# When four finished rows are normalised during the last matrix product, and which sum each later row's norm follows

## The chip, the cores and the metric

The kernel runs on one core of one Trainium2 chip. TensorE (PE) multiplies matrices into PSUM banks, VectorE (DVE), ScalarE (ACT) and GpSimd (POOL) work on SBUF tiles, SyncE (SP) and ACT issue the stores. Each engine executes its own instruction list in order and waits on semaphores of the others. The metric is device time in microseconds (us) of the whole program.

## The reference

Two blocks over 1024 tokens of width 1024 are computed one after the other; the second ends in a wide feed-forward product and a norm over each row:

```
h = h + jnp.square(jax.nn.relu(m @ w_up[l])) @ w_down[l]
...
h = rms_norm(h, norm_final)

def rms_norm(x, g):
    xf = x.astype(jnp.float32)
    y = xf * lax.rsqrt(jnp.mean(xf * xf, axis=-1, keepdims=True) + EPS)
    return (y * g.astype(jnp.float32)).astype(x.dtype)
```

Only the end matters here: the sums into h for the last quarter of `w_down`, and the final norm.

## The kernel before

The output h lies in SBUF as `X`, eight row tiles (t = 0 to 7, called rows here) of 128 tokens by 1024 columns, each in two column halves (ch = 0 and 1). The product with `w_down` is done in seven sub-products for each of four parts of its inner dimension (loop over `c`); each sub-product goes to four PSUM banks, 128 by 512 each, one for each row of a half of the tokens. A float32 operand is split into a high and a low part: `whi` by ACT (L118, a cast), `wlo` by POOL (L119, a subtraction), and three matmuls (L108, L110, L111) are done for each pair of blocks. In `times` a bank takes 12 matmuls; with `by_t` set, as in the last two sub-products, one bank is finished after the other and the banks of the last sub-product are the same four as those of the one before.

`into(banks, h, ch, done)` adds four banks to `X` (L2034, on DVE). In the last part `done` says that a half row is complete, and `half_done` then squares it and adds up the squares on ACT into `fin` (L1987), and multiplies it in place by the gains `nf` on POOL (L1989). Only half ch = 0 of row 7 is not multiplied there.

`finish(t, n)` takes n rows that are complete: DVE adds the two halves' sums of squares (L1994) and works out the reciprocal root by Newton steps, a chain of small instructions on 128 by n elements that each need the one before: L141 (`hx`), L124 (`r`), then three rounds of `w` and `r`. For n = 4 a round has three instructions (L130, L131, L132), for n = 1 two (L128, L132). ACT then scales each row (L1999) and SP stores it. Row 7 is scaled half by DVE (L2002), half by ACT (L2005), and stored from SP and ACT.

The last part's order is: rows 0 to 3, half 1 (whose half 0 was done earlier); rows 4 to 7, half 1; rows 4 to 7, half 0. The recording layer (`tc`) sets the order of the instructions on each engine; `tc.issue_after(ins)` gives the instructions inside it a place behind `ins`. How the instructions of two steps interleave on DVE and ACT is decided there, and is read from the built instruction lists.

Of the kernel before, what the change touches and what calls it, by code (L numbers as in the profile page):

```python
# [22 lines left out]
NT = T // P  # L23
# [7 lines left out]
def fused_kernel(tc, a, out, stop=None, dbg=None):  # L31
# [85 lines left out]
    def split_evac(hi, lo, src, lo_eng=None):  # L117
        nc.scalar.copy(out=hi, in_=src)  # L118
        return (lo_eng or nc.vector).tensor_tensor(out=lo, in0=src, in1=f(hi), op=ALU.subtract)  # L119
# [18 lines left out]
    def rsqrt(ss, n, rows=P):  # L138

        hx, r, w_ = small3(ss.shape[-1])  # L140
        nc.vector.tensor_scalar(out=hx[:rows], in0=ss[:rows], scalar1=0.5 / n, scalar2=0.5 * EPS, op0=ALU.mult,  # L141
                                op1=ALU.add)
        newton(hx[:rows], r[:rows], w_[:rows])
        return r
# [75 lines left out]
    added, loads, made = [None], [None], [None]  # L220
# [7 lines left out]
    def load_d(dst, w, j, n, c=0, qs=(0, 2)):  # L228

        for i in range(2):  # L230
            q = 4 * c + qs[i]
            loads[:] = [nc.sync.dma_start(out=dst[i], in_=w[:, q:q + 2, j, n * 512:n * 512 + 512])]
        return dst
# [9 lines left out]
    def split_into(t_, parts):  # L243

        for i in range(2):
            made[:] = [split_evac(t_[:, 2 * i:2 * i + 2, :], t_[:, 4 + 2 * i:6 + 2 * i, :], parts[i])]
        return t_
# [15 lines left out]
    def banks4():  # L263
        return [bank() for _ in range(4)]
# [264 lines left out]
    with lay:  # L529
# [267 lines left out]
        for h in range(2):  # L797
# [8 lines left out]
            for i in range(4):  # L806
                t = 4 * h + i
# [35 lines left out]
    with ExitStack() as ph:  # L843
# [191 lines left out]
        def load_x(h, ch):  # L1035
            for t in range(4 * h, 4 * h + 4):
                nc.sync.dma_start(out=X.at(t, ch), in_=d_x1[t][:, ch * 512:ch * 512 + 512])
# [108 lines left out]
        for n, ks in enumerate(((), (), (), (0, 1, 2), (3, 4), (5, 6), (7,), ())):  # L1146
            t = [n % 4]
# [21 lines left out]
        for k in range(KT):  # L1169
            ps = turned(X.x[4:], k)  # L1170
            h, l = x2.at(k, slice(NM + 512, TM))
# [7 lines left out]
        last = scaled  # L1179
# [231 lines left out]
    with ExitStack() as ph:  # L1411
# [65 lines left out]
        class Head:  # L1477
# [145 lines left out]
            def finish(self, hf):  # L1623
                hh, y = self.hh, self.t["y", hf]
                tp = pst.tile([P, 512], F32, name="tp")
                for ch in range(4):
                    nc.tensor.transpose(tp[:, ch * P:(ch + 1) * P], y[:, ch * P:(ch + 1) * P], ident)
                sl = slice(hf * H, hf * H + H)
                oh_ = gp.tile([P, H], F32, name="oh")
                nc.vector.scalar_tensor_tensor(out=oh_, in0=tp, scalar=gn[:, hh:hh + 1], in1=self.t["gs", 0][:, sl],  # L1630
                                               op0=ALU.mult, op1=ALU.mult)
                if hh < 3:
                    nc.sync.dma_start(out=d_hg[hh][:, sl], in_=oh_)
                else:
                    split_evac(*oo.at(7, sl), oh_)
# [53 lines left out]
        last = []  # L1689
        for hh in range(3):  # L1690
# [6 lines left out]
            last = head.ends()  # L1697
# [54 lines left out]
    with ExitStack() as ph:  # L1752
# [106 lines left out]
        for n, ks in enumerate(((), (), (0, 1, 2), (3, 4), (5, 6), (7,), (), ())):  # L1859
            t = [n % 4]  # L1860
# [29 lines left out]
    def load_a(n):  # L1890
        if n < len(seq):
            c, s_ = seq[n]
            nc.sync.dma_start(out=blocks[n % 3], in_=d_u[s_][:, 4 * c:4 * c + 4, :])
# [77 lines left out]
    with ExitStack() as ph:  # L1971
        bb = ph.enter_context(tc.tile_pool(name="bb", bufs=4, reuse_waits="tile"))
        X = ph.enter_context(tc.tile_pool(name="xpool3", bufs=1, reuse_waits="tile")).tile([P, NT, D], F32, name="X3")
        ba = ph.enter_context(tc.tile_pool(name="ba", bufs=1, side="right", reuse_waits="tile"))
        blocks.append(ba.tile([P, 4, 512], F32, name="ub"))
        nf = ba.tile([P, D], F32, name="nf")
        fin = {}

        def half_done(t, ch):

            g = t if t >= 4 else 0
            if g not in fin:
                fin[g] = st.tile([P, 8], F32, name="fin", bufs=5)
            csl = slice(ch * 512, ch * 512 + 512)
            i = 4 * ch + (t if t < 4 else 0)
            junk = st.tile([P, 1024], BF16, name="junk", bufs=1)
            nc.scalar.activation(out=junk[:, csl], in_=X[:, t, csl], func=AF.Square, accum_out=fin[g][:, i:i + 1])  # L1987
            if (t, ch) != (NT - 1, 0):
                nc.gpsimd.tensor_tensor(out=X[:, t, csl], in0=X[:, t, csl], in1=nf[:, csl], op=ALU.mult)  # L1989

        def finish(t, n):

            ss = fin[t]
            nc.vector.tensor_tensor(out=ss[:, :n], in0=ss[:, :n], in1=ss[:, 4:4 + n], op=ALU.add)  # L1994
            r = rsqrt(ss[:, :n], D)
            for i in range(n):
                tsl = slice((t + i) * P, (t + i + 1) * P)
                if t < NT - 1:
                    nc.scalar.activation(out=X[:, t + i, :], in_=X[:, t + i, :], func=AF.Copy, scale=r[:, i:i + 1])  # L1999
                    nc.sync.dma_start(out=out[tsl, :], in_=X[:, t + i, :])  # L2000
                else:
                    nc.vector.scalar_tensor_tensor(out=X[:, t, :512], in0=X[:, t, :512], scalar=r, in1=nf[:, :512],  # L2002
                                                   op0=ALU.mult, op1=ALU.mult)
                    nc.sync.dma_start(out=out[tsl, :512], in_=X[:, t, :512])
                    nc.scalar.activation(out=X[:, t, 512:], in_=X[:, t, 512:], func=AF.Copy, scale=r)  # L2005
                    nc.scalar.dma_start(out=out[tsl, 512:], in_=X[:, t, 512:])

        def load_w21(c):
            return load_d([bb.tile([P, 2, 512], F32, name="wb") for _ in range(2)], wd, 1, 0, c)

        def load_x(h, ch):
            for t in range(4 * h, 4 * h + 4):
                nc.sync.dma_start(out=X[:, t, ch * 512:ch * 512 + 512], in_=d_x[t][:, ch * 512:ch * 512 + 512])

        def split_n(n):
            t_ = split_into(xt.tile([P, KT, 512], F32R, name=("xh0", "xl0", "xl1")[n % 3]),
                            [blocks[n % 3][:, 2 * i:2 * i + 2, :] for i in range(2)])
            load_a(n + 3)
            return t_

        w21 = load_w21(0)
        w12, w22 = load_w2(0)

        store(loads[0].ins)
        load_x(0, 0)
        load_a(2)
        load_x(0, 1)
        load_x(1, 1)
        load_x(1, 0)

        def into(banks, h, ch, done=False):
            for t in range(4):
                dst = X[:, 4 * h + t, ch * 512:ch * 512 + 512]
                added[:] = [nc.vector.tensor_tensor(out=dst, in0=dst, in1=banks[t], op=ALU.add)]  # L2034
                if done:
                    half_done(4 * h + t, ch)
                    if h and not ch:
                        finish(4 * h + t, 1)

        def operands(n, b_):  # L2040
            return split_n(n), split_b(b_)


        ops = operands(0, w11)
        for c in range(NCH):
            n, last = 7 * c, c == NCH - 1
            B, A_ = banks4(), banks4()
            times(B, *ops, True)
            ops = operands(n + 1, w21)
            less(w12, w12, w22)  # L2050
            into(B, 0, 0)
            times(A_, *ops, True)
            less(w11, w11, w12)
            ops = operands(n + 2, w11)
            into(A_, 0, 0, last)
            times(B, *ops, False)
            less(w21, w21, w11)
            less(w11, w22, w11)
            ops = operands(n + 3, w11)
            into(B, 0, 1)  # L2060
            C = banks4()
            times(C, *ops, True)
            ops = operands(n + 4, w22)
            if not last:
                w11 = load_w11(wd, c + 1)
                w21_ = load_w21(c + 1)
            if c == NCH - 2:
                nc.sync.dma_start(out=nf, in_=a["norm_final_2"].partition_broadcast(P))
            into(C, 1, 1)
            times(C, *ops, False)  # L2070
            ops = operands(n + 5, w12)
            if not last:
                w12, w22 = load_w2(c + 1)
            into(C, 0, 1, last)
            times(B, *ops, False, last)
            ops = operands(n + 6, w21)
            into(B, 1, 1, last)
            if last:
                with tc.issue_after(added[0].ins):
                    finish(0, 4)  # L2080
            times(B, *ops, False, last)
            if not last:
                w21 = w21_
                ops = operands(n + 7, w11)
            into(B, 1, 0, last)
# [26 lines left out]
```

## Time and profile before

| what | value |
|---|---|
| median of 3 runs | 2329.97 us (2328.25 to 2332.85) |
| profiled execution, its time | 2328.69 us |
| its span, first to last instruction | 2326.9 us |
| PE busy | 2258.1 us (97%), 11782 matmuls |
| DVE busy | 1520.7 us (65%) |
| ACT busy | 1033.2 us (44%) |
| POOL busy | 735.0 us (32%) |
| mean granted TensorE clock | 0.993 |

The profiled execution is 1.28 us below the median and 1.79 us longer than its span. Busy shares are means over the whole program; the change touches the last 35 us alone, so the timeline of that stretch is what is read below. In a row of the timeline stand the start (us from the span's start), the duration of the group, engine, line, operation, output and inputs, shapes, the number of instructions merged in the row, and in brackets the engine's idle time before it with what ended it.

### The profile page before, as it was taken

What the parts mean: (1) busy time and instruction counts of PE and PEld (TensorE: products, weight loads), DVE (VectorE), ACT (ScalarE), POOL (GpSimd) and SP (SyncE); (2) the same over time, 40 slices, a digit from 0 to 9 for tenths busy, and PEclk for the clock granted to TensorE, in tenths of its full rate; (3) what the DMA queues carried; (4) which work ended last, traced back from release to release, by engine and by line L of the source; (5) the groups of instructions that cost most, each with busy time, mean ns of one, the idle gap of its engine ahead of it and who ended that gap; (6) DMA issues with size and microseconds to landing.
All of it is one profiled execution on the core that took longest, in us unless ns stands there. A gap on an engine that the chain in (4) does not pass through costs nothing.

```text
span 2326.9 us, 32033 instructions
## 1 busy us (share of the span) xinstructions
PE 2258.1 (97%) x11782; PEld 1902.9 (82%) x11782; DVE 1520.7 (65%) x2768; ACT 1033.2 (44%) x1943; POOL 735.0 (32%) x513
## 2 busy tenths in 40 slices
PE   7999999989999999999999999999999999999997
PEld 6888888767787888878988888888878888878886
DVE  5577786798698354553265746759895444787775
ACT  5355552643356354453233232423565555533334
POOL 2112133344501442431312112121024444544455
PEclk9999999999999999999999999999999999999999
DMA  4312113423362311211111111358245444754231
GB/s 144 75 28 55 28 35 108 142 75 123 113 246 101 93 44 50 56 64 42 55 46 55 42 55 51 131 185 300 89 147 194 152 151 159 276 217 163 100 127 73
DMA packets 249581, 255.17 MB, mean 110 GB/s; under 512 B 61193, under 2 KB 183135, under 8 KB 245585
## 3 DMA queue, kind: packets, MB, share of 16 engines
q1 hardware_dynamic: 240608, 235.48, 31.3%
q10 hardware_dynamic: 8224, 16.00, 1.8%
q0 software_dynamic: 592, 1.65, 0.3%
q8 instruction: 93, 1.52, 0.3%
q14 instruction: 64, 0.52, 0.1%
HBM read 181.26 MB, written 69.46 MB: 108 GB/s over the span
## 4 chain that ended last, share of the span: by engine, by line
PE 61%; DVE 10%; issue 3%; DMA 3%; ACT 2%; SPq 0%; POOL 0%; DVEq 0%; ACTq 0%; POOLq 0%
PE mm L110 18%; PE mm L111 18%; PE mm L108 18%; PE A L1564 2%; PE PT L1328 1%; DVE sum L226 1%; DVE xl L119 1%; PE S L1305 1%; PE tp L1584 1%; DVE s L1317 1%; DVE X L2034 0%; DVE r L132 0%; DMA wb<-in_w_down_dram 0%; DVE wlo L119 0%; DVE z L226 0%
## 5 line engine op out<-in xcount | busy, mean ns | idle before, releaser
L108 PE MATMUL mm<-xh,whi 128*128 128x512 f32 (+2 forms) x1616 | 622.6, 386 | 12.1 <-DVE z L226 4.8
L110 PE MATMUL mm<-xl,whi 128*128 128x512 f32 (+2 forms) x1616 | 616.2, 381 | 0.0
L111 PE MATMUL mm<-xh,wlo 128*128 128x512 f32 (+2 forms) x1616 | 613.0, 379 | 0.2 <-POOL wlo L80 0.2
L80 POOL TENSOR_TENSOR wlo<-wraw,whi 128x1024 fp32r<-128x1024 f32 (+1 forms) x99 | 233.7, 2364 | 856.7 <-ACT whi L79 672.7
L108 PEld LDWEIGHTS mm<-xh,whi 128*128 128x128 f32 x1616 | 306.2, 190 | 70.4 <-DVE z L226 5.6
L111 PEld LDWEIGHTS mm<-xh,wlo 128*128 128x128 f32 x1616 | 306.3, 190 | 58.4 <-POOL wlo L80 0.5
L110 PEld LDWEIGHTS mm<-xl,whi 128*128 128x128 f32 x1616 | 306.5, 190 | 50.6
L111 PE MATMUL mm<-whi,xl 128*128 128x512 f32 (+1 forms) x752 | 271.2, 361 | 0.0
L79 ACT CAST whi<-wraw 128x1024 fp32r<-128x1024 f32 (+1 forms) x99 | 101.2, 1023 | 253.3 <-PE mm L110 139.0
L110 PE MATMUL mm<-wlo,xh 128*128 128x512 f32 (+1 forms) x560 | 196.8, 351 | 2.7 <-POOL wlo L80 1.4
L108 PE MATMUL mm<-whi,xh 128*128 128x512 f32 (+1 forms) x560 | 196.5, 352 | 1.8 <-DVE x L527 1.0
L108 PE MATMUL mm<-whi,xl 128*128 128x512 f32 x416 | 162.2, 390 | 1.8 <-DVE X L2034 1.8
L110 PE MATMUL mm<-wlo,xl 128*128 128x512 f32 x416 | 162.1, 390 | 1.2 <-DVE wlo L119 1.2
L111 PEld LDWEIGHTS mm<-whi,xl 128*128 128x128 f32 x752 | 141.7, 188 | 21.6
L276 POOL TENSOR_TENSOR wlo<-raw,whi 128x1024 fp32r<-128x1024 f32 (+1 forms) x59 | 123.0, 2087 | 114.4 <-ACT whi L275 111.7
L110 PEld LDWEIGHTS mm<-wlo,xh 128*128 128x128 f32 x560 | 105.7, 189 | 17.8 <-POOL wlo L80 2.0
L108 PEld LDWEIGHTS mm<-whi,xh 128*128 128x128 f32 x560 | 105.7, 189 | 16.7 <-DVE x L527 1.4
L276 POOL TENSOR_TENSOR wlo<-wraw,whi 128x1024 fp32r<-128x1024 f32 (+1 forms) x28 | 71.9, 2569 | 120.2 <-ACT whi L275 85.9
L2034 DVE TENSOR_TENSOR X<-X,mm 128x512 f32<-128x512 f32 x112 | 73.1, 681 | 37.8 <-PE mm L111 37.8
L1313 DVE CUSTOM_DVE_ANT_0 s<-S,bi 128x400 f32<-128x400 f32 x64 | 34.5, 571 | 95.2 <-PE S L1305 95.2
L108 PEld LDWEIGHTS mm<-whi,xl 128*128 128x128 f32 x416 | 78.1, 188 | 19.2 <-ACT whi L118 1.8
L226 DVE TENSOR_TENSOR st<-st 128x512 f32<-128x512 f32 x64 | 62.6, 999 | 46.9 <-ACT st L1958 45.8
(441 smaller groups left out, 4594.3 us busy)
## 6 DMA issues: line engine op xcount, KB each, us to landing
wraw<-in_w_in_dram SPq DMA_DIRECT2D x48, 512.0 KB, 3.6
d_S<-st SPq DMA_DIRECT2D x64, 256.0 KB, 4.6
raw<-in_w_up_dram SPq DMA_DIRECT2D x30, 512.0 KB, 5.2
d_A<-st ACTq DMA_DIRECT2D x48, 256.0 KB, 2.0
fa<-d_S SPq DMA_DIRECT2D x10, 1024.0 KB, 4.7
fa<-d_A SPq DMA_DIRECT2D x9, 1024.0 KB, 4.7
wraw<-in_attn_w_in_dram SPq DMA_DIRECT2D x32, 256.0 KB, 3.0
xh<-in_w_down_dram SPq DMA_DIRECT2D x16, 512.0 KB, 5.7
```

The costliest lines, as they stand in the source:

```text
L79: nc.scalar.copy(out=hv[:, i:i + n], in_=view[:, i:i + n])
L80: nc.gpsimd.tensor_tensor(out=lv[:, i:i + n], in0=view[:, i:i + n], in1=f(hv[:, i:i + n]), op=ALU.subtract)
L108: nc.tensor.matmul(ps, lhsT=lh[0], rhs=rh[0], start=first and i == 0, stop=False, skip_group_check=chain)
L110: nc.tensor.matmul(ps, lhsT=lh[0], rhs=rh[1], start=False, stop=False, skip_group_check=chain)
L111: nc.tensor.matmul(ps, lhsT=lh[1], rhs=rh[0], start=False, stop=last and i == n - 1, skip_group_check=chain)
L119: return (lo_eng or nc.vector).tensor_tensor(out=lo, in0=src, in1=f(hi), op=ALU.subtract)
L226: return nc.vector.tensor_tensor(out=out_, in0=x_, in1=y_, op=op)
L276: nc.gpsimd.tensor_tensor(out=lv, in0=view, in1=f(hv), op=ALU.subtract)
L1305: nc.tensor.matmul(sps[j], lhsT=(ql if n == 2 else qh)[rows, qsl], rhs=(kl if n == 1 else kh)[rows, ksl], start=n == 0, stop=n == 2)
L1313: nc.vector.tensor_tensor_reduce(out=s, in0=sps[j], in1=bs[j], scale=-0.125, scalar=-NEG, op0=ALU.add, op1=ALU.min, accum_out=mx)
L1564: nc.tensor.matmul(aps[:, ch, :], lhsT=kc[:, ch * P:(ch + 1) * P], rhs=pat(Q, ch * P, n, nbc), start=True, stop=True)
L2034: added[:] = [nc.vector.tensor_tensor(out=dst, in0=dst, in1=banks[t], op=ALU.add)]
```

## The change

`finish(0, 4)` for rows 0 to 3 stood behind the four sums of rows 4 to 7, half 1, and gets its place ahead of them, behind the last split of an operand (`made[0]`). And in the last `into` a row's `finish` is no longer called straight behind its own sum, but tied behind the sum of the next row; row 7's stays at the end.

```
--- before.py
+++ after.py
@@ into
                 added[:] = [nc.vector.tensor_tensor(out=dst, in0=dst, in1=banks[t], op=ALU.add)]
                 if done:
                     half_done(4 * h + t, ch)
-                    if h and not ch:
-                        finish(4 * h + t, 1)
+                    if h and not ch and t:
+
+                        with tc.issue_after(added[0].ins):
+                            finish(4 * h + t - 1, 1)
+            if done and h and not ch:
+                finish(NT - 1, 1)
@@ the loop over c
             ops = operands(n + 6, w21)
+            if last:
+                with tc.issue_after(made[0].ins):
+                    finish(0, 4)
             into(B, 1, 1, last)
-            if last:
-                with tc.issue_after(added[0].ins):
-                    finish(0, 4)
             times(B, *ops, False, last)
```

The instruction lists of PE, POOL and SP keep their order; DVE's and ACT's change. On DVE this stood behind the last operand split (`xh` from `fa`); the eight sums are rows 0 to 3 and rows 4 to 7, both half 1, and the chain of 128x4 that follows belongs to rows 0 to 3.

```order
L119 TENSOR_TENSOR xh_20142<-fa,xh_20142 128x1024 x2
L2034 TENSOR_TENSOR X_18185<-X_18185,mm 128x512 x8
L1994 TENSOR_TENSOR fin<-fin 128x4
L141 TENSOR_SCALAR hx_20176<-fin 128x4
L124 TENSOR_SCALAR r_20177<-hx_20176 128x4
L130 TENSOR_TENSOR w_20178<-r_20177 128x4
```

In the changed kernel the same place reads:

```order
L119 TENSOR_TENSOR xh_20142<-fa,xh_20142 128x1024 x2
L2034 TENSOR_TENSOR X_18185<-X_18185,mm 128x512 x4
L1994 TENSOR_TENSOR fin<-fin 128x4
L141 TENSOR_SCALAR hx_20156<-fin 128x4
L124 TENSOR_SCALAR r_20157<-hx_20156 128x4
L130 TENSOR_TENSOR w_20158<-r_20157 128x4
L131 TENSOR_TENSOR w_20158<-w_20158,hx_20156 128x4
L132 SCALAR_TENSOR_TENSOR r_20157<-w_20158,r_20157 128x4
L130 TENSOR_TENSOR w_20158<-r_20157 128x4
L2034 TENSOR_TENSOR X_18185<-X_18185,mm 128x512
L131 TENSOR_TENSOR w_20158<-w_20158,hx_20156 128x4
L132 SCALAR_TENSOR_TENSOR r_20157<-w_20158,r_20157 128x4
```

The chain has moved ahead of the sum of row 4, half 1, which now stands behind its first seven instructions; its last five stand behind that sum, and then follow five sums (rows 5, 6, 7 of half 1 and rows 4, 5 of half 0).

On ACT the end of the program before was this; the first `whi` is the first half of the last weight block, the second `whi` its second half, and the squares (L1987) come in the order rows 0 to 7 of half 1, then rows 4 to 7 of half 0.

```order
L1987 ACTIVATE junk,fin<-X_18185 128x512 x3
L118 CAST whi<-wb 128x1024
L1987 ACTIVATE junk,fin<-X_18185 128x512 x4
L118 CAST whi<-wb 128x1024
L1987 ACTIVATE junk,fin<-X_18185 128x512
L1999 ACTIVATE X_18185<-X_18185,r_20177 128x1024 x4
L1987 ACTIVATE junk,fin<-X_18185 128x512 x3
L1999 ACTIVATE X_18185<-X_18185,r_20252 128x1024
```

And in the changed kernel:

```order
L1987 ACTIVATE junk,fin<-X_18185 128x512 x3
L118 CAST whi<-wb 128x1024
L1987 ACTIVATE junk,fin<-X_18185 128x512 x2
L1999 ACTIVATE X_18185<-X_18185,r_20157 128x1024 x4
L1987 ACTIVATE junk,fin<-X_18185 128x512 x2
L118 CAST whi<-wb 128x1024
L1987 ACTIVATE junk,fin<-X_18185 128x512 x3
L1999 ACTIVATE X_18185<-X_18185,r_20256 128x1024
```

The four scalings of rows 0 to 3 have moved from behind the second `whi` to ahead of the squares of rows 5 and 6, half 1, and so ahead of the second `whi`.

At the end of DVE's list of the changed kernel a row's whole chain (nine instructions of 128x1) stands between two sums; here is row 4's chain between the sums of rows 5 and 6, half 0:

```order
L1994 TENSOR_TENSOR fin<-fin 128x1
L141 TENSOR_SCALAR hx_20255<-fin 128x1
L124 TENSOR_SCALAR r_20256<-hx_20255 128x1
L128 SCALAR_TENSOR_TENSOR w_20257<-r_20256,hx_20255 128x1
L132 SCALAR_TENSOR_TENSOR r_20256<-w_20257,r_20256 128x1
L128 SCALAR_TENSOR_TENSOR w_20257<-r_20256,hx_20255 128x1
L132 SCALAR_TENSOR_TENSOR r_20256<-w_20257,r_20256 128x1
L128 SCALAR_TENSOR_TENSOR w_20257<-r_20256,hx_20255 128x1
L132 SCALAR_TENSOR_TENSOR r_20256<-w_20257,r_20256 128x1
L2034 TENSOR_TENSOR X_18185<-X_18185,mm 128x512
```

Before, the sum of row 6 stood behind the first four instructions of row 4's chain, and the sum of row 7 behind the rest of rows 4, 5 and most of row 6. Now row 4's chain stands between the sums of rows 5 and 6, row 5's between those of rows 6 and 7, and row 6's behind the sum of row 7, mixed with row 7's.

## Rows read from the trace of the kernel before

**Rows 1.** Timeline of PE in the last 35 us: first matmul of the last sub-product, the seventh (first that reads the second half of the weight block), the eighth, and the last of all.

```profile
2301.91 0.39 PE L108 MATMUL mm<-whi,xh 128*128 128x512 f32 x1
...
2303.27 0.39 PE L108 MATMUL mm<-whi,xh 128*128 128x512 f32 x1
2304.65 0.50 PE L110 MATMUL mm<-wlo,xh 128*128 128x512 f32 x1 [1.00 <-POOL wlo L119]
...
2313.88 0.39 PE L111 MATMUL mm<-whi,xh 128*128 128x512 f32 x1
```

**Rows 2.** Timeline of ACT: end of the square of row 3, half 1; the square of row 6, half 1, and the cast behind it; the four scalings of rows 0 to 3; two squares behind them.

```profile
2292.77 0.19 ACT L1987 ACTIVATION_READ_ACCUMULATOR junk<-X 128x1 f32 x1
...
2300.17 0.63 ACT L1987 ACTIVATE junk<-X 128x512 bf16<-128x512 f32 x1 [2.00 <-DVE X L2034]
...
2300.80 1.05 ACT L118 CAST whi<-wb 128x1024 fp32r<-128x1024 f32 x1
...
2307.94 4.27 ACT L1999 ACTIVATE X<-X,r 128x1024 f32<-128x1024 f32 x4 [4.32 <-DVE r L132]
2312.12 0.61 ACT L1987 ACTIVATE junk<-X 128x512 bf16<-128x512 f32 x1
...
2312.85 0.63 ACT L1987 ACTIVATE junk<-X 128x512 bf16<-128x512 f32 x1
```

**Rows 3.** Timeline of POOL: multiplications by the gains (L1989) of rows 0 to 2; low part of the first half of the last weight block; rows 3 and 4; row 5; low part of the second half; row 7, all of half 1.

```profile
2289.33 3.80 POOL L1989 TENSOR_TENSOR X<-X,nf 128x512 f32<-128x512 f32 x3
...
2293.09 2.40 POOL L119 TENSOR_TENSOR wlo<-wb,whi 128x1024 fp32r<-128x1024 f32 x1
2295.44 2.54 POOL L1989 TENSOR_TENSOR X<-X,nf 128x512 f32<-128x512 f32 x2
2298.25 1.29 POOL L1989 TENSOR_TENSOR X<-X,nf 128x512 f32<-128x512 f32 x1 [0.26 <-ACT junk L1987]
...
2302.22 2.38 POOL L119 TENSOR_TENSOR wlo<-wb,whi 128x1024 fp32r<-128x1024 f32 x1
2304.55 1.29 POOL L1989 TENSOR_TENSOR X<-X,nf 128x512 f32<-128x512 f32 x1
```

**Rows 4.** Timeline of DVE: sums of rows 4 and 5, half 1; the first two instructions and the last of the chain of rows 0 to 3.

```profile
2293.95 0.69 DVE L2034 TENSOR_TENSOR X<-X,mm 128x512 f32<-128x512 f32 x1 [2.03 <-PE mm L111]
2296.67 0.69 DVE L2034 TENSOR_TENSOR X<-X,mm 128x512 f32<-128x512 f32 x1 [2.03 <-PE mm L111]
...
2302.71 1.91 DVE L1994 TENSOR_TENSOR fin<-fin 128x4 f32<-128x4 f32 x1
2304.65 1.22 DVE L141 TENSOR_SCALAR hx<-fin 128x4 f32<-128x4 f32 x1
...
2307.68 0.17 DVE L132 SCALAR_TENSOR_TENSOR r<-w,r 128x4 f32<-128x4 f32 x1
```

**Rows 5.** Timeline of DVE and POOL behind the sum of row 5, half 0: the wait of row 4's chain, POOL's multiplications of rows 4 and 5 and of row 6, the sum of row 6, three chain instructions that took long, and the sum of row 7.

```profile
2312.85 0.16 DVE L1994 TENSOR_TENSOR fin<-fin 128x1 f32<-128x1 f32 x1 [3.30 <-ACT junk L1987]
2312.90 2.52 POOL L1989 TENSOR_TENSOR X<-X,nf 128x512 f32<-128x512 f32 x2 [7.06 <-ACT junk L1987]
...
2313.43 0.78 DVE L128 SCALAR_TENSOR_TENSOR w<-r,hx 128x1 f32<-128x1 f32 x1
2314.13 0.67 DVE L2034 TENSOR_TENSOR X<-X,mm 128x512 f32<-128x512 f32 x1
2314.72 0.71 DVE L132 SCALAR_TENSOR_TENSOR r<-w,r 128x1 f32<-128x1 f32 x1
...
2315.70 1.26 POOL L1989 TENSOR_TENSOR X<-X,nf 128x512 f32<-128x512 f32 x1 [0.28 <-ACT junk L1987]
2315.72 1.25 DVE L132 SCALAR_TENSOR_TENSOR r<-w,r 128x1 f32<-128x1 f32 x1
...
2318.71 0.68 DVE L2034 TENSOR_TENSOR X<-X,mm 128x512 f32<-128x512 f32 x1
```

**Rows 6.** Timeline of PE at its two longest waits in the middle of the program, with the matmul with which each ends and the first that starts at the short distance again behind the second one.

```profile
483.00 0.50 PE L111 MATMUL mm<-s2h,wlo 128*128 128x512 f32 x1 [2.50 <-POOL u L895]
...
516.63 0.79 PE L108 MATMUL mm<-xh,whi 128*128 128x512 f32 x1 [3.73 <-DVE z L226]
...
522.70 0.40 PE L111 MATMUL mm<-s2h,wlo 128*128 128x512 f32 x1
```

**Rows 7.** Stretches behind those waits: length, busy time of PE, PEld, DVE, ACT and POOL with the number of instructions, granted clock of TensorE (1.00 is 2.4 GHz, 0.50 is 1.2 GHz), DMA share, GB/s.

```profile
483.00:487.00 4.00, 4.00 (x17) 3.30 (x18) 4.00 (x5) 1.20 (x2) 2.76 (x1) 1.00 0.00 0
...
515.80:522.60 6.80, 5.97 (x14) 4.71 (x15) 6.77 (x8) 3.70 (x5) 2.74 (x4) 0.50 0.00 0
```

**Rows 8.** The end of the program: row 7's chain on DVE (its first and its sixth instruction, and row 7's scaling), the scaling of row 6 on ACT and ACT's last store; and the rate of all DMA engines in 40 slices of the last 7 us, 2320 to 2327.

```profile
2320.23 1.13 ACT L1999 ACTIVATE X<-X,r 128x1024 f32<-128x1024 f32 x1
2320.35 0.16 DVE L1994 TENSOR_TENSOR fin<-fin 128x1 f32<-128x1 f32 x1 [0.64 <-ACT junk L1987]
...
2321.38 0.22 DVE L128 SCALAR_TENSOR_TENSOR w<-r,hx 128x1 f32<-128x1 f32 x1
...
2322.27 0.75 DVE L2002 SCALAR_TENSOR_TENSOR X<-X,r,nf 128x512 f32<-128x512 f32 x1
2323.02 0.37 ACTq L2006 DMA_DIRECT2D out_dram<-X  x1
...
GB/s 492 398 421 445 398 398 398 421 468 374 398 211 187 445 445 374 398 421 421 304 24 23 281 410 433 410 398 398 421 270 0 0 0 0 0 0 0 0 0 0
```

## The prediction

> **What bounds the kernel now.** I read the chain of waits first: up to 2302 us it is PE alone, and then it leaves PE for DVE's and ACT's norms. So I read the last 35 us engine by engine. PE's last sub-product starts at 2301.91; its seventh matmul reads the second half of the weight block, and the eighth needs that block's low part, which POOL finishes at 2304.60 [rows 3]. So PE stood still 1.00 us, and its last matmul starts at 2313.88 and ends at 2314.27 [rows 1]. Matmuls of a dense run follow each other by 0.227 us (six steps from 2301.91 to 2303.27), so a bank of 12 takes 2.72 us.
>
> What follows PE's end is late for another reason. The sum of row 7 could start at 2314.3 and starts at 2318.71 [rows 5], 4.4 us late: ACT's four scalings lie in the way of the squares of rows 7 and 4 [rows 2], row 4's chain waits 3.30 us for such a square, and the sums of rows 6 and 7 are queued behind it on DVE. From the sum of row 7 to the span's end it is 8.2 us. The change aims at these 4.4 us.
>
> One more thing must be seen. While POOL works, many of DVE's small instructions stand still. The chain's first, 128x4, took 1.91 us and ended at 2304.62, when POOL's subtraction ended (2304.60); the second took 1.22 us, to 2305.87, and POOL's next multiplication ended at 2305.84. The ten behind it, with POOL idle, took 0.2 us each (2305.87 to 2307.85) [rows 3, 4]. It happens for one column too: 0.78, 0.71 and 1.25 us, each up to the end of a multiplication on POOL [rows 5].
>
> **Rows 0 to 3 moved forward.** The chain can start when the square of row 3 is done, at 2292.96 [rows 2]. POOL is then at the end of rows 0 to 2 (2293.13), goes on with the low part of the first half (to 2295.49) and row 3 (to 2296.71) [rows 3]. So I let the first instruction through at 2293.1, hold the second to 2295.5 and the third to 2296.7. POOL's next work, row 4, needs the sum of row 4, which now stands behind seven instructions of this chain; POOL is idle and the four left take 0.8 us. So the sum of row 4 starts at 2297.5 and not at 2293.95 [rows 4]. If POOL held nothing, it would start at 2294.4; if the chain's first instruction were also held, at 2298.0.
>
> From there on ACT decides. Behind the sum come five chain instructions, the first 0.6 us behind its start (as 2314.13 to 2314.72, [rows 5]), and ACT starts scaling 0.09 us behind the last (2307.85 to 2307.94): at 2297.5 + 0.6 + 4 x 0.2 + 0.17 + 0.09 = 2299.2. The next four steps take their distances from [rows 2]: four scalings, 4.18 us to the next instruction; the square of row 5 at 2303.35; that of row 6 0.73 us later, 2304.1; the second `whi` 0.63 us behind that, 2304.7, done at 2305.75. It was done at 2301.85.
>
> POOL's list is unchanged: row 5, row 6, then the second low part. POOL starts 0.78 us behind a square (2312.12 to 2312.90, [rows 2, 5]) and takes 1.27 us for a row: row 5 from 2304.1, row 6 to 2306.65, and the low part, 2.4 us, to 2309.0 [rows 3]. PE's eighth matmul then starts at 2309.05 and not at 2304.65. **The stall costs +4.4 us**, since all that PE has left, 41 matmuls or 9.6 us, is behind it. Nothing hides it: PE's list holds only this sub-product. With POOL holding nothing the same sum gives 2306.0, +1.35.
>
> **The clock.** Between 2303.4 and 2309.05 PE would have one matmul. A wait of 3.73 us was followed by a granted clock of 0.50, 1.2 GHz, from 515.8 to 522.6; one of 2.50 us by 1.00 [rows 6, 7]. At 0.50 the 14 steps from 516.63 to 522.70 took 6.07 us; at 0.227 they are 3.18, so 2.9 us were lost, 0.2 for each step. The slow stretch began 2.9 us behind the last matmul (512.90) and lasted 6.8. Put the same behind 2303.4 and it ends at 2313.1, 4.0 us into the rest, 9 slow steps, 1.9 us; put it behind the lone matmul, which ends near 2306, and it ends near 2315.5, 6.4 us, 15 slow steps, 3.0 us. **I take +2.5 us**, with 0 (the 2.50 us row) and 3.0 as bounds.
>
> The Trainium skill, "TensorE: Matmul & The Clock Gate", section "HAM oscillation — how this bites in real kernels", says that a wait of PE between two bursts lets the second start at the low clock. That speaks against this change; the trace agrees for 3.73 us and not for 2.50 us. [...]
>
> **Rows 4 to 7 tied behind the next sum.** This takes the 4.4 us away: no sum waits for a square now. But a whole chain lies between two sums. Row 4's starts 0.6 us behind the sum of row 5, its sixth instruction 1.03 us later (2320.35 to 2321.38, [rows 8]), at 1.62 us; POOL's multiplication of row 5 starts 1.58 us behind that sum (2296.67 to 2298.25, [rows 3, 4]) and holds the chain to 2.85 us. The rest takes 0.65 us (of the 0.89 from 2321.38 to 2322.27, less the held one's own 0.2), so the sum of row 6 starts 3.5 us behind that of row 5. The next step is alike, 3.5 us with row 6's multiplication. The banks come every 2.72 us, so the sum of row 7 is 2 x 3.5 - 2 x 2.72 = 1.55 us late behind its bank. Bounds are 0 (nothing held) and 1.8. **The change gains 4.4 - 1.55 = 2.85 us here.**
>
> **The end.** Row 7's chain now shares DVE with row 6's, 0.1 us. Row 6's scaling ended at 2321.36 and the last stores were issued at 2323.02, 1.66 us later [rows 8]; now row 6's root is ready only behind row 7's sum, and the scaling ends about 0.7 us ahead of the last stores. Its 512 KB take 1.25 us at some 420 GB/s [rows 8], so the last stores queue for 0.55 us. **+0.65 us**, from 0 to 0.8. The stores of rows 0 to 3, four more DMAs, leave SP's queue some 9 us earlier, when nothing else is stored: no price.
>
> **Sum.** 4.4 + 2.5 - 2.85 + 0.65 = +4.7 us. Against the profiled execution, 2328.69, that is 2333.4; against the median, 2329.97, it is 2334.7, or +0.20%. I take 0.2% (4.66 us) as what a measurement of this kernel can tell from no change. The forecast lies on that line, by a hair on its slower side.
>
> **The rivals.**
> 1. *The norm gets through early.* If POOL's work holds none of DVE's chain, the scaling starts at 2296.05, the stall is +1.35 us, PE's wait is too short for the clock and no sum is late: 1.35 - 4.4 + 0.65 = -2.4 us, 2327.6, faster; with rows 4 and 5 held as above, 2329.1. For it: nothing but that the durations of POOL are rough. Against: the same two instructions were held in the trace. Chance 0.08, both prices.
> 2. *The clock stays at 1.00*, since a lone matmul breaks the wait and 2.50 us did nothing: 2334.7 - 2.5 = 2332.2. Chance 0.13.
> 3. *Rows 4 and 5 aren't held*, because their multiplications start later than the chain's end: row 7's sum follows its bank, 2334.7 - 1.55 = 2333.2. Against: they would have to start 0.9 us later, 2.5 us behind the sum. Chance 0.10.
> 4. *The chain's last step is caught.* The last instruction of rows 0 to 3 starts 1.4 us behind the sum of row 4, POOL's row 4 at 1.58. If POOL starts more than 0.18 us earlier or DVE is later by that, the step waits for 1.27 us and the scaling, the low part and PE with it: 2334.7 + 1.25 = 2335.95, clearly slower. Chance 0.17. The Trainium skill, "SBUF — State Buffer", section "Who interferes with whom", says that whichever of the two starts first has the port pair for its whole instruction; by that a margin of 0.18 us is enough. The trace has no such near case.
>
> The forecast has the 0.52 that is left; its own range is 2333.2 to 2336.2 (0.7 us for the slow stretch, 0.5 for the start of row 4's sum, 0.4 for the end).
>
> **How the numbers follow.** Slower by over 0.2%, above 2334.63: about six tenths of the forecast (0.31), nearly all of the fourth (0.16), a little of the second and third (0.03): 0.50. Faster by over 0.2%, below 2325.3: only the first's better end with a fast run, 0.03. Within: 0.47. The range leaves out most of the first case and the far tails: 2328.5 to 2337.5.
>
> **What would show it.** Second `whi` behind four scalings, near 2304.7; PE's longest wait of the end on the low part near 2309, over 2 us in one piece; granted clock near 0.5 behind it and matmuls 0.43 us apart; sums of rows 5, 6 and 7, half 0, over 3 us apart with a `w` or `r` of over 0.7 us between them; last sum near 2322.8. The forecast is wrong if the scalings start before 2297, if PE's eighth matmul starts before 2306, or if the clock is 1.00 to the end.

## The result, and the profile after

The changed kernel takes 2333.48 us, median of 20 runs (2327.9 to 2336.3); the kernel before, run beside it, 2329.03 us (20 runs). The ratio is 1.0017, with a 95% interval of 1.0011 to 1.0024: slower by about 4 us (4.45 between the medians). The profiled execution took 2334.18 us with a span of 2332.4 us.

Where in the program does it come from? In the two profiled executions the first matmul of the last sub-product starts at 2301.91 and at 2302.71. In all ten profiled executions of this study it lies between 2300.48 and 2304.36, and in none of them does PE wait from 2270 us up to it: the moved steps, which begin some 9 us ahead of it, do not reach PE before it. That spread belongs to the program before, and it is why a single time says little here. So **stage times below are counted from that matmul**, and each is that of one execution. To the end of the span it is 24.99 us before and 29.69 us after: +4.70 us, all in the last sub-product and what follows it.

PE after, as [rows 1]: the first matmul of the last sub-product, the sixth, the seventh (second `whi`), the eighth (second `wlo`), the first at the short distance again, the last.

```profile
2302.71 0.39 PE L108 MATMUL mm<-whi,xh 128*128 128x512 f32 x1
...
2303.84 0.39 PE L111 MATMUL mm<-whi,xh 128*128 128x512 f32 x1
2306.55 0.50 PE L108 MATMUL mm<-whi,xh 128*128 128x512 f32 x1 [2.32 <-ACT whi L118]
2309.73 0.79 PE L110 MATMUL mm<-wlo,xh 128*128 128x512 f32 x1 [2.68 <-POOL wlo L119]
...
2315.28 0.39 PE L111 MATMUL mm<-whi,xh 128*128 128x512 f32 x1
...
2321.42 0.39 PE L111 MATMUL mm<-whi,xh 128*128 128x512 f32 x1
```

One wait of 1.00 us has become two, 2.32 and 2.68 us, with a lone matmul between. The stretches behind them (length, busy time of PE, PEld, DVE, ACT, POOL, granted clock, DMA share, GB/s):

```profile
2309.70:2315.00 5.30, 5.27 (x12) 4.13 (x13) 0.69 (x1) 0.72 (x2) 2.36 (x2) 0.50 0.00 0
2315.00:2321.80 6.80, 6.80 (x30) 5.29 (x28) 4.91 (x18) 2.49 (x5) 1.43 (x2) 0.99 0.00 0
```

The first 5.3 us of what was left ran at half the clock. Timeline of ACT, DVE and POOL ahead of that, as [rows 2 to 4]: the norm of rows 0 to 3, the scalings, and what stands behind them.

```profile
2293.79 0.17 DVE L1994 TENSOR_TENSOR fin<-fin 128x4 f32<-128x4 f32 x1 [1.08 <-ACT junk L1987]
2293.90 2.40 POOL L119 TENSOR_TENSOR wlo<-wb,whi 128x1024 fp32r<-128x1024 f32 x1
2294.00 2.33 DVE L141 TENSOR_SCALAR hx<-fin 128x4 f32<-128x4 f32 x1
2296.25 1.30 POOL L1989 TENSOR_TENSOR X<-X,nf 128x512 f32<-128x512 f32 x1
2296.36 1.21 DVE L124 TENSOR_SCALAR r<-hx 128x4 int32<-128x4 int32 x1
...
2298.28 0.68 DVE L2034 TENSOR_TENSOR X<-X,mm 128x512 f32<-128x512 f32 x1
...
2299.66 0.16 DVE L132 SCALAR_TENSOR_TENSOR r<-w,r 128x4 f32<-128x4 f32 x1
...
2299.86 1.29 POOL L1989 TENSOR_TENSOR X<-X,nf 128x512 f32<-128x512 f32 x1 [2.31 <-ACT junk L1987]
2299.92 4.28 ACT L1999 ACTIVATE X<-X,r 128x1024 f32<-128x1024 f32 x4
...
2304.88 2.50 POOL L1989 TENSOR_TENSOR X<-X,nf 128x512 f32<-128x512 f32 x2 [3.73 <-ACT junk L1987]
2305.47 1.03 ACT L118 CAST whi<-wb 128x1024 fp32r<-128x1024 f32 x1
2307.34 2.34 POOL L119 TENSOR_TENSOR wlo<-wb,whi 128x1024 fp32r<-128x1024 f32 x1
```

`hx` ends with POOL's subtraction (2296.33 beside 2296.30), `r` with its next multiplication (2297.57 beside 2297.55). Then four scalings, two squares, and only then the second `whi`; POOL's two multiplications and the low part follow, to 2309.68.

The end, as [rows 5]: sums of rows 5, 6 and 7 of half 0, the held step of each chain between them with the multiplication that holds it, row 7's square and scaling, and ACT's last store.

```profile
2316.41 0.69 DVE L2034 TENSOR_TENSOR X<-X,mm 128x512 f32<-128x512 f32 x1 [3.45 <-PE mm L111]
...
2317.99 1.30 POOL L1989 TENSOR_TENSOR X<-X,nf 128x512 f32<-128x512 f32 x1 [2.86 <-ACT junk L1987]
2318.03 1.27 DVE L128 SCALAR_TENSOR_TENSOR w<-r,hx 128x1 f32<-128x1 f32 x1
...
2319.86 0.68 DVE L2034 TENSOR_TENSOR X<-X,mm 128x512 f32<-128x512 f32 x1
...
2321.88 1.26 POOL L1989 TENSOR_TENSOR X<-X,nf 128x512 f32<-128x512 f32 x1 [2.60 <-ACT junk L1987]
2321.92 1.24 DVE L128 SCALAR_TENSOR_TENSOR w<-r,hx 128x1 f32<-128x1 f32 x1
...
2323.27 0.68 DVE L2034 TENSOR_TENSOR X<-X,mm 128x512 f32<-128x512 f32 x1
...
2324.50 0.61 ACT L1987 ACTIVATE junk<-X 128x512 bf16<-128x512 f32 x1
...
2327.24 0.75 DVE L2002 SCALAR_TENSOR_TENSOR X<-X,r,nf 128x512 f32<-128x512 f32 x1
...
2328.06 0.35 ACTq L2006 DMA_DIRECT2D out_dram<-X  x1
```

The sums are 3.45 and 3.41 us apart. PE's last matmul ends at 2321.81, so row 7's sum is 1.46 us late; before it was 4.44 us late.

For the experiments, the same places in all ten kernels. The column of the first matmul of the last sub-product counts from the span's start; all others are starts (for the span, its end) less that (us):

| kernel | first matmul | eighth | last | sum of row 5 | row 6 | row 7 | end of span |
|---|---|---|---|---|---|---|---|
| before | 2301.91 | 2.74 | 11.97 | 6.95 | 12.22 | 16.80 | 24.99 |
| after | 2302.71 | 7.02 | 18.71 | 13.70 | 17.15 | 20.56 | 29.69 |
| first_only | 2301.60 | 7.02 | 17.67 | 13.01 | 16.45 | 19.87 | 27.80 |
| ties_only | 2300.48 | 2.75 | 11.99 | 6.97 | 12.23 | 16.47 | 25.32 |
| after_nomult | 2304.36 | 7.02 | 18.86 | 13.83 | 16.57 | 19.29 | 28.04 |
| after_filled | 2302.78 | 7.13 | 16.33 | 11.32 | 14.77 | 18.17 | 27.22 |
| after_late | 2304.24 | 3.54 | 12.73 | 7.72 | 11.17 | 14.57 | 23.66 |
| first_late | 2303.22 | 3.54 | 12.74 | 7.73 | 11.69 | 15.11 | 23.08 |
| pipe_late | 2301.80 | 3.54 | 12.78 | 7.77 | 10.49 | 13.30 | 22.90 |
| pipe_early | 2302.43 | 1.58 | 10.65 | 5.64 | 9.29 | 12.58 | 22.17 |

### The profile page after: what moved, and what is told of

Its sections match the earlier page's. It is cut to its first block, busy times and chain, and to the rows that moved or that the text cites. A ratio compares the mean times of both kernels' runs of the same rounds, so it can differ in the third digit from the quotient of the medians.

```text
span 2332.4 us, 32029 instructions
## 1 busy us (share of the span) xinstructions
PE 2260.4 (97%) x11782; PEld 1904.5 (82%) x11782; DVE 1523.5 (65%) x2768; ACT 1033.7 (44%) x1943; POOL 735.1 (32%) x513
## 3 DMA queue, kind: packets, MB, share of 16 engines
q0 software_dynamic: 592, 1.65, 0.3%
## 4 chain that ended last, share of the span: by engine, by line
PE 62%; DVE 9%; issue 3%; DMA 2%; ACT 2%; POOL 1%; SPq 0%; DVEq 0%; ACTq 0%; POOLq 0%
PE mm L110 19%; PE mm L111 18%; PE mm L108 18%; PE A L1564 2%; PE PT L1328 1%; DVE sum L226 1%; PE S L1305 1%; PE tp L1584 1%; DMA xh<-in_w_down_dram 1%; DVE s L1317 1%; DVE xl L119 1%; DMA wraw<-in_w_na_out_dram 0%; ACT whi L118 0%; DVE wlo L119 0%; DVE z L226 0%
```

## The experiments

### first_only: rows 0 to 3 moved, the later norms as before

```
             ops = operands(n + 6, w21)
+            if last:
+                with tc.issue_after(made[0].ins):
+                    finish(0, 4)
             into(B, 1, 1, last)
-            if last:
-                with tc.issue_after(added[0].ins):
-                    finish(0, 4)
```

> Only rows 0 to 3 are moved forward; each later row's norm stays behind its own sum. All numbers count from the first matmul of the last sub-product to the end of the span: 25.0 us before, 29.7 us with both parts. Theory A (as the prediction put it): the tie of the later norms is what takes the 4.4 us of late sums away, so without it the stall (+4.3) and the slow clock (+2.5) come on top of before: about 31.8 us. Theory B: what made the sums late were the four scalings of rows 0 to 3 ahead of the squares on ACT; with the scalings gone from there, the sums are late only by the steps of the chains, and the tie brings next to nothing: about 29.3 us, the sum of row 7 about 21 us behind the first matmul (20.6 with both parts).

Measured: 27.80 us (2331.2 us in its one run, beside 2329.86 of the kernel before). Timeline of DVE, sums of rows 5, 6 and 7 and row 7's scaling:

```profile
2314.61 0.68 DVE L2034 TENSOR_TENSOR X<-X,mm 128x512 f32<-128x512 f32 x1
...
2318.05 0.68 DVE L2034 TENSOR_TENSOR X<-X,mm 128x512 f32<-128x512 f32 x1
...
2321.47 0.68 DVE L2034 TENSOR_TENSOR X<-X,mm 128x512 f32<-128x512 f32 x1
...
2324.92 0.75 DVE L2002 SCALAR_TENSOR_TENSOR X<-X,r,nf 128x512 f32<-128x512 f32 x1
```

Theory A falls: without any tie the sums are 3.44 and 3.42 us apart, as with it, and row 7's comes at 19.87, 1.81 us behind the end of PE's last matmul (4.44 before, 1.46 with both parts). What had made them late was the four scalings ahead of the squares on ACT. The end is 1.5 us earlier than theory B gave, for two reasons. The slow clock cost less in this execution: the 41 matmuls from the eighth to the last took 10.65 us here and 11.69 with both parts; no run shows why. And the end behind row 7's sum is 7.93 us, where theory B had 8.3; with the tie it is 9.13.

### ties_only: the later norms tied, rows 0 to 3 as before

```
-                    if h and not ch:
-                        finish(4 * h + t, 1)
+                    if h and not ch and t:
+
+                        with tc.issue_after(added[0].ins):
+                            finish(4 * h + t - 1, 1)
+            if done and h and not ch:
+                finish(NT - 1, 1)
```

> Only the later norms are tied behind the next row's sum; rows 0 to 3 stay where they were. Counted as before (25.0 us before, 29.7 with both parts). Theory A: no sum waits for a square any more, 2.85 us less and 0.65 at the end: about 22.8 us. Theory B: row 4's chain still stands ahead of row 6's sum on DVE and waits for the square that stands behind the four scalings; only row 7's sum comes ahead of row 6's chain: 24.3 to 25.0 us. Both: PE's eighth matmul at 2.7 us, no slow clock.

Measured: 25.32 us, 0.33 more than before (2327.62 us in its one run). Timeline of DVE: row 4's chain begins, the sums of rows 6 and 7, row 7's scaling.

```profile
2311.43 0.16 DVE L1994 TENSOR_TENSOR fin<-fin 128x1 f32<-128x1 f32 x1 [3.29 <-ACT junk L1987]
...
2312.71 0.67 DVE L2034 TENSOR_TENSOR X<-X,mm 128x512 f32<-128x512 f32 x1
...
2316.95 0.68 DVE L2034 TENSOR_TENSOR X<-X,mm 128x512 f32<-128x512 f32 x1
...
2320.87 0.75 DVE L2002 SCALAR_TENSOR_TENSOR X<-X,r,nf 128x512 f32<-128x512 f32 x1
```

The chain still waits 3.29 us for a square, as in [rows 5], with the sum of row 6 queued behind it. Row 7's sum comes 0.33 us earlier, and the end behind it is 8.85 us and not 8.19. The tie alone gains nothing on the whole; theory A's 22.8 us falls, and theory B's 25.0 was 0.3 us short.

### after_nomult: no multiplication on POOL in half 0 of rows 4 to 6

```
-            if (t, ch) != (NT - 1, 0):
+            if ch or t < 4:
                 nc.gpsimd.tensor_tensor(out=X[:, t, csl], in0=X[:, t, csl], in1=nf[:, csl], op=ALU.mult)
```

> The changed kernel without POOL's multiplication by the gains in half 0 of rows 4 to 6 (these rows' half 0 stays without gains: a part of the computation is left out). Theory of the held chain: no chain instruction behind the sums of rows 5 and 6 takes over 0.3 us, these sums and row 7's stand 2.7 us apart as the banks come, and row 7's sum follows its bank at once: 1.4 us less, 28.2 us from the first matmul of the last sub-product to the end. Rival, that a chain of nine steps is itself what takes 3.4 us between two sums: still 3.4 us apart, 29.7 us. Stall and clock are the same in both.

Measured: 28.04 us (2334.24 us in its one run, whose first matmul comes 1.65 us later than in the changed kernel's trace). Timeline of DVE, sums of rows 5 to 7 and the step that was held:

```profile
2318.19 0.69 DVE L2034 TENSOR_TENSOR X<-X,mm 128x512 f32<-128x512 f32 x1 [3.58 <-PE mm L111]
...
2319.81 0.22 DVE L128 SCALAR_TENSOR_TENSOR w<-r,hx 128x1 f32<-128x1 f32 x1
...
2320.93 0.69 DVE L2034 TENSOR_TENSOR X<-X,mm 128x512 f32<-128x512 f32 x1 [0.25 <-PE mm L111]
...
2323.65 0.69 DVE L2034 TENSOR_TENSOR X<-X,mm 128x512 f32<-128x512 f32 x1 [0.24 <-PE mm L111]
```

The same step takes 0.22 us and not 1.27, the sums are 2.74 and 2.72 us apart, and each waits for PE. So it is POOL's multiplication that holds the chain, not the chain's own length. The Trainium skill, "SBUF — State Buffer", section "Who interferes with whom", says just that for a VectorE instruction with two SBUF inputs beside a GpSimd one that reads SBUF; the trace agrees, 1.27 beside 0.22 us.

### after_filled: PE's wait filled with matmuls that nobody reads

```
-            times(B, *ops, False, last)
+            times(B, *ops, False, last, fill=bank() if last else None)
...
+            if fill is not None and (i, t) == (1, 0): [nc.tensor.matmul(fill, lhsT=s_[:, 0, tsl], rhs=w_[0][0][:, 0, :], start=True, stop=True, skip_group_check=True) for _ in range(24)]
```

> The changed kernel with 24 more matmuls of the same shape into an unused PSUM bank, between the sixth and the seventh matmul of the last sub-product, where PE would wait; their results are not read. Theory of the clock: PE's wait is filled, the granted clock stays at 1.00, the matmuls behind it follow each other by 0.23 us and not by 0.43, PE's last matmul comes 2.4 us earlier; the sum of row 7 is then about 18 us behind the first matmul (20.6) and the end 27.1 us (29.7). The wait itself stays: the first matmul that needs the second low part starts at 7.0 us. Rival, that the slow steps come from the work beside them (ACT's and POOL's) and not from the wait: 0.43 us steps as before and 29.7 us.

Measured: 27.22 us (2331.85 us in its one run). The stretches from the filled wait on, columns as above, and the eighth matmul:

```profile
2304.00:2309.00 5.00, 5.00 (x24) 4.14 (x23) 0.00 (x0) 3.17 (x8) 4.04 (x3) 1.00 0.61 251
2309.00:2316.00 7.00, 7.00 (x32) 5.51 (x31) 2.42 (x8) 1.45 (x4) 3.71 (x4) 1.00 0.00 0
```

```profile
2309.91 0.50 PE L110 MATMUL mm<-wlo,xh 128*128 128x512 f32 x1
```

The eighth matmul still comes late, at 7.13 us, but the granted clock is 1.00 all through, and the last matmul comes at 16.33 us and not at 18.71. POOL and ACT do the same beside it, so the slow steps came from the wait. Between these two executions the clock's share of the loss is 29.69 - 27.22 = 2.47 us.

### after_late: the four scalings behind the second whi

```
-        nc.scalar.copy(out=hi, in_=src)
+        cast[:] = [nc.scalar.copy(out=hi, in_=src)]
...
-                    nc.scalar.activation(out=X[:, t + i, :], in_=X[:, t + i, :], func=AF.Copy, scale=r[:, i:i + 1])
+                    with tc.issue_after(cast[0].ins) if n > 1 else ExitStack(): nc.scalar.activation(out=X[:, t + i, :], in_=X[:, t + i, :], func=AF.Copy, scale=r[:, i:i + 1])
```

> Both parts of the change, and the four scalings of rows 0 to 3 tied on ACT behind the second whi; nothing else. Theory of the order on ACT: the second whi is done near 0.2 us behind the first matmul of the last sub-product (2.8 with the change), the second low part near 3.5, PE's eighth matmul near 3.55 (7.0 with the change, 2.7 before), granted clock 1.00; the squares of rows 4 to 7, half 0, still find ACT free; sums of rows 5, 6, 7 are 3.4 us apart, that of row 7 near 14.5 (20.6), the end near 23.6 us (29.7 with the change, 25.0 before): some 1.4 us faster than before. Rival, that the four scalings now stand in the way of the squares as they did before: sum of row 7 near 17.5, end near 26 us.

Measured: 23.66 us in the trace; 2328.6 us, ratio to the kernel before 0.9998 (0.999 to 1.0007). The second cast on ACT, the scalings, PE's eighth matmul and the sum of row 7:

```profile
2303.43 1.03 ACT L118 CAST whi<-wb 128x1024 fp32r<-128x1024 f32 x1
2304.37 4.26 ACT L1999 ACTIVATE X<-X,r 128x1024 f32<-128x1024 f32 x4
...
2307.78 0.50 PE L110 MATMUL mm<-wlo,xh 128*128 128x512 f32 x1 [1.79 <-POOL wlo L119]
...
2318.81 0.68 DVE L2034 TENSOR_TENSOR X<-X,mm 128x512 f32<-128x512 f32 x1
```

One tie on ACT takes 6.0 us off the end of the changed kernel in the traces, and about 4.4 us by the ratios of the runs (1.0017 and 0.9998): PE's eighth matmul is at 3.54 us, and behind its wait of 1.79 us the matmuls follow each other by 0.23 us, at a granted clock of 1.00. In the trace this is 1.33 us better than before; the runs can't tell it from no change.

### first_late: the same without the tie of the later norms

The edits of first_only and after_late together.

> Only rows 0 to 3 moved forward, with their scalings tied behind the second whi; the later norms as before. The theory that the tie of the later norms brings nothing: PE as in the run beside it (eighth matmul near 3.55), row 7's sum a little later, near 15.2, but a shorter end behind it, 7.9 us and not 9.1: near 23.2 us, as fast as with the tie or faster. Rival, that the tie is worth its 1.5 us once PE isn't late: near 25 us.

Measured: 23.08 us; 2327.72 us, ratio 0.9991 (0.9983 to 1.0). Row 7's sum is at 15.11, 0.54 us later than with the tie, and the end behind it 7.97 us and not 9.09. With PE late by only 0.8 us the tie is still worth nothing: by the two traces it costs 0.6 us, which the runs (intervals 0.9983 to 1.0 and 0.999 to 1.0007) do not tell apart.

### pipe_late and pipe_early: chains cut in two

```
+                with tc.issue_after(half[0].ins) if done and h and not ch and t > 1 else ExitStack():
+                    added[:] = [nc.vector.tensor_tensor(out=dst, in0=dst, in1=banks[t], op=ALU.add)]
...
+                        with tc.issue_after(added[0].ins):
+                            if t > 1:
+                                finish(4 * h + t - 2, 1, "b")
+                            if t:
+                                finish(4 * h + t - 1, 1, "a")
```

Part "a" is a chain's first five steps, "b" its last four with the scaling; `half` is the last step of "a". pipe_late has this beside the edit of after_late. pipe_early has it with, in place of that edit, a tile of its own for the second half of the last weight block, whose cast is tied behind the first's.

> As the first of these runs, and each later row's chain cut in two on DVE: its first five steps ahead of the next row's sum, its last four behind it, so that POOL's multiplication falls where the sum is waited for. Expected: sums of rows 5, 6, 7 as far apart as the banks come, 2.7 us, row 7's sum at its bank near 13.2 us behind the first matmul of the last sub-product, and a slightly longer end, 9.1 to 9.3 us, since three chains now end there: 22.4 us, 2.6 us faster than before. Rival, that the held steps only move behind the last sum: end of 10.5 us or more, 23.7 us as without the cut.

> Chains cut in two as in the run beside it, and the second half of the last weight block split into a tile of its own right behind the first half, so that nothing on ACT or POOL can hold PE in the last sub-product: eighth matmul at 1.6 us (2.7 before), PE's last at 10.6. The price: POOL does the second low part ahead of row 4 and holds the chain of rows 0 to 3 for 2.4 us more, the scalings start 2.3 us later and meet the squares of half 0. By that row 7's sum comes near 13 us and the end near 22 us; were the scalings hidden, 11 and 20 us.

Measured, pipe_late: 22.90 us; 2327.96 us, ratio 0.9994 (0.9983 to 1.0005). DVE from the sum of row 6 to that of row 7:

```profile
2312.29 0.69 DVE L2052 TENSOR_TENSOR X<-X,mm 128x512 f32<-128x512 f32 x1 [1.14 <-PE mm L111]
2312.89 0.21 DVE L2009 SCALAR_TENSOR_TENSOR w<-r,hx 128x1 f32<-128x1 f32 x1
...
2313.91 1.26 DVE L2010 SCALAR_TENSOR_TENSOR r<-w,r 128x1 f32<-128x1 f32 x1
2315.10 0.68 DVE L2052 TENSOR_TENSOR X<-X,mm 128x512 f32<-128x512 f32 x1
```

A step is still held, but nearly all of it falls where the sum would have waited for PE anyway: the sums are 2.72 and 2.81 us apart. The end behind row 7's is 9.60 us, more than the 9.1 to 9.3 expected, so it ends at 22.90 us and not at 22.4. The extra time lies behind the issue of the stores: ACT's last store is issued 4.55 us behind that sum (4.79 in the changed kernel), but from there to the end of the span it is 5.05 us (4.34).

Measured, pipe_early: 22.17 us; 2326.36 us, ratio 0.9989 (0.9981 to 0.9998): **faster than the kernel before**, by some 2.6 us, though the interval, 0.5 to 4.4 us, ends just short of no change. The changed kernel, at 1.0017 of the kernel before, is slower than both. PE has no wait in its last sub-product; its eighth matmul is at 1.58 us. The price is the expected one:

```profile
2297.20 2.42 POOL L119 TENSOR_TENSOR xl<-wb,xl 128x1024 fp32r<-128x1024 f32 x1
...
2297.34 2.31 DVE L130 TENSOR_TENSOR w<-r 128x4 f32<-128x4 f32 x1
...
2301.78 4.28 ACT L2016 ACTIVATE X<-X,r 128x1024 f32<-128x1024 f32 x4
...
2306.75 6.28 POOL L1989 TENSOR_TENSOR X<-X,nf 128x512 f32<-128x512 f32 x5 [3.72 <-ACT junk L1987]
```

The second low part holds the chain for another 2.31 us, the scalings run to 2306.06, and POOL does five multiplications in one piece behind them, so row 7's sum is 1.54 us late behind its bank (10.65 + 0.39 = 11.04, and 12.58).

## Why the prediction was right, and where it was not

The forecast was +0.20%, with 0.50 for slower by more than that and 0.47 for within it; the measured change is +0.17%, and its interval reaches both sides of the 0.2% line. Step by step, each counted from the first matmul:

- **Start of row 4's sum, half 1.** Forecast 2297.5, that is 4.4 us ahead of the first matmul; measured 4.43. The chain's second and third instruction were held as taken; the near case of the fourth rival did not occur, with a margin of 0.20 us (2299.66 and 2299.86). The prediction said that the trace before has no near case, but [rows 5] has two: a step that starts 0.05 us ahead of POOL (2312.85) takes 0.16 us, and one that starts 0.02 us behind it (2315.72) takes 1.25. So the order decided there at margins far below the 0.18 us of this rival.
- **The stall.** Forecast +4.4 us; measured 7.02 - 2.74 = +4.28. The scalings, the squares, the cast and POOL's work each came within 0.15 us. (The squares that the scalings hold up in the kernel before are of rows 4 and 5, half 0; the prediction says rows 7 and 4. No number hangs on it.)
- **The clock.** Forecast +2.5 us; measured 11.69 - 9.23 = +2.46 in the changed kernel, +1.42 in first_only and +2.61 in after_nomult with the same waits. The lone matmul did not save it: waits of 2.32 and 2.68 us with one matmul between were followed by 0.50, while the single wait of 2.50 us in [rows 6] was not. The second rival falls. That the clock would fall was argued from [rows 6, 7]; that the size came out to 0.04 us is luck, since the three executions differ by 1.2 us.
- **The held chains.** Forecast: 3.5 us between sums, row 7's 1.55 us late; measured 3.45 and 3.41, and 1.46. after_nomult shows the cause; the third rival falls.
- **Where the gain comes from: wrong.** The prediction said of the tie of rows 4 to 7 that "this takes the 4.4 us away". It does not: ties_only still has the wait for the square, and first_only has lost it. Of the gain of 2.98 us (4.44 - 1.46), 2.63 us stay in first_only without the tie (4.44 - 1.81): they belong to moving rows 0 to 3, whose scalings on ACT stood ahead of the squares. The prediction had itself named these scalings as the reason and then booked the gain to the other edit. The sum was not touched by it, since both edits were made together.
- **The end: too small.** Forecast +0.65 us; measured 9.13 - 8.19 = +0.94. It is the tie's price: without it the end is 7.93 us. Behind the issue of ACT's last store it is 4.34 us and not 3.88, +0.46, where 0.55 was forecast; ahead of it 4.79 us and not 4.31, +0.48, where 0.1 was forecast for DVE alone. The prediction left out ACT: row 7's square stands behind row 5's scaling there and starts 1.23 us behind its sum, where it was 0.91 before (2319.62). Over the three pairs of kernels with and without the tie it brings row 7's sum nearer to PE's last matmul by 0.3 to 0.5 us and makes the end 0.7 to 1.2 us longer: a net loss each time.

The four terms as measured: 4.28 + 2.46 - 2.98 + 0.94 = +4.70 us, the difference of the two traces. That the sum meets the forecast of +4.7 to the digit is luck too: the end was 0.29 us too small, the stall and the gain each 0.12 to 0.13 us off the other way.

That the stall, and not the moved norm as such, is what makes the change slow is shown by after_late: the same early chain, its scalings behind one cast, ends 6.0 us earlier. Of the 4.28 us, 3.48 go with the scalings (7.02 - 3.54); the other 0.80 stay, since the early chain still delays the sum of row 4, half 1, and by it the squares, the cast and POOL's low part.

## What to carry to other kernels

When a step is moved forward, look at every engine it issues to and ask what now stands behind it there: here the chain on DVE cost PE 0.8 us, and the four scalings on ACT held a cast on which PE's operands hung and cost it 3.5 us. Book a gain to the edit that removes its cause, and try each edit alone: of this pair one held nearly all the gain and the stall, the other a small net loss. PE's wait here cost 1.4 to 2.6 us more than its length, since the clock fell behind it; shortening the wait (after_late) or filling it (after_filled) kept the clock at 1.00.

## What the runs showed of the hardware that was not expected

Two waits of 2.32 and 2.68 us around a single matmul lowered the granted clock as one wait of 3.73 us did, and the same waits cost 2.46, 1.42 and 2.61 us in three executions; in first_only the matmuls were slow only over the first seven steps behind the wait, in the changed kernel over twelve. No run shows what makes the difference.

Small DVE instructions with one input in SBUF behaved differently by width: `hx` and `r` of 128x4 were held 2.33 and 1.21 us by POOL, while in the kernel before the same two of 128x1 at 2313.05 and 2313.24 took 0.15 us each while POOL's multiplications of [rows 5] were running:

```profile
2313.05 0.15 DVE L141 TENSOR_SCALAR hx<-fin 128x1 f32<-128x1 f32 x1
2313.24 0.15 DVE L124 TENSOR_SCALAR r<-hx 128x1 int32<-128x1 int32 x1
```

That POOL holds the wide ones is read from the ends, which meet POOL's within 0.03 us; widths other than 4 and 1 were not run.
